# Second pair of attention heads ahead of retention, output projection cut along other tiles

## The chip, the cores and the metric

The kernel runs on one core of a Trainium2 chip. The metric is the device time of one execution in microseconds. Five engines take part: PE (TensorE, matrix products; PEld is its weight load), DVE (VectorE), ACT (ScalarE), POOL (GpSimd) and SP (SyncE, which issues nearly all DMAs). Each engine works through its own queue of instructions in order.

## The reference

Two layers over 512 tokens of width 1024, in float32. Each layer is a SwiGLU, a mixer and a second SwiGLU. The mixer projects the normalised tokens once and feeds four mixers of width 256, whose outputs are joined and projected by `w_out`:

```python
for l in range(DEPTH):
    x = x + 0.5 * swiglu(rmsnorm(x, ffn1_norm[l]), ffn1_w_gate[l], ffn1_w_up[l], ffn1_w_down[l])
    h = rmsnorm(x, mix_norm[l])
    u = h @ w_in[l]
    ...
    y_conv = short_conv_mixer(c_x, c_b, c_c, conv_w[l])
    y_rwkv = rwkv7_mixer(rw_r, rw_k, rw_v, ...)
    y_ret = retention_mixer(rt_q, rt_k, rt_v, rt_g, positions, ret_gn_g[l])
    y_mla = mla_mixer(ml_qa, ml_kva, positions, ...)
    x = x + jnp.concatenate([y_conv, y_rwkv, y_ret, y_mla], axis=-1) @ w_out[l]
    x = x + 0.5 * swiglu(rmsnorm(x, ffn2_norm[l]), ffn2_w_gate[l], ffn2_w_up[l], ffn2_w_down[l])
```

`rwkv7_mixer` is a recurrence over the tokens in both directions, `retention_mixer` a decayed attention in chunks with a normalisation at its end, `mla_mixer` a softmax attention of four heads.

## The kernel before

Activations lie feature by feature: a tile is 128 features by 512 tokens, and x is eight such tiles. Every large product is made of three products of rounded parts (`mm3`, L341): a weight block is split into a high and a low part (`split`, L326: one ACT copy, one DVE subtraction), and so is an activation (`y_split`, L638). The joined mixer output is eight tiles: 0 and 1 convolution, 2 and 3 RWKV, 4 and 5 retention, 6 and 7 attention. The weights `wo` of the output projection are stored in the order of `WOUT`, that is 0, 1, 4, 5, 2, 3, 6, 7.

`Mixers.run` (L552) writes the parts down in this order: the RWKV inputs and inverse, the RWKV recurrence (`rwkv_chain`, L1161), then everything that has nothing to do with it: the latents, the inputs of retention, the convolution, the inputs of attention, heads 0 and 1 (`mla(0)`), retention, the normalisation of the RWKV output (`rwkv_norm`, L1264), x brought back from DRAM (`x_back`, L590), the normalisation of retention (`retention_end`, L784), heads 2 and 3 (`mla(1)`), the RWKV output turned round (`rwkv_out`, L1295), and the output projection in two halves: weight columns 0 to 3, which are convolution and retention, and then 4 to 7, which are RWKV and attention.

The recurrence has eight steps. One step is a string of short products on PE with DVE or ACT between them: scores (L1187) and mask (L1191), old state (L1206), values (L1209), a copy (L1213), the solve (L1218), a negated copy (L1221), the new state (L1233, L1242, L1243), outputs (L1251, added by L1258).

One head of `mla` (L894) makes four score tiles (L909), each followed by a maximum and a scaling on DVE (L911, L912), an exponential on ACT (L914), a reciprocal and a scaling on DVE (L915, L916); then 16 transposes (L921) and copies (L922). The products with the values of both heads come after that (L929).

The order in which instructions stand in the engines' queues isn't the order of the source. It is planned when the kernel is built: of the instructions that could start, the one written earlier goes first, so that the parts written after `rwkv_chain` fill its waits; `in_turn` (L579) and `issue_after` pin an order, and the splits of weights carry a higher priority (`AHEAD`, L330). Tiles come from rings of buffers, one ring for each tag: SBUF has `v` (19 buffers), `f` (23), `h` (8) and `w_raw` (3); PSUM has `mm` (3), `a` (2) and `b` (3). The plan hands out the buffers of one ring in the order in which the source first writes the tiles: a tile never takes its buffer before a tile of the same ring that is written earlier in the source. The tags of `mla` are one line (scores, transposes, values of each head):

```python
MLA_TAGS = (("mm", "mm", "mm"), ("mm", "mm", "mm"), ("b", "a", "mm"), ("b", "a", "mm"))   # L28
```

The recurrence takes its scores and transposes from `a` and its products `zy` from `b`. Retention takes all its PSUM tiles from `mm`, its masked scores `ret_ms` from `f`, and two of the three `w_raw` buffers for each of its two halves (`ret_big`, `ret_big2`: decay tables, states). The attention output `m_y` and the transposed weights `m_pT` come from `f`.

Of the kernel before, what the change touches and what calls it, by code (L numbers as in the profile page):

```python
# [9 lines left out]
F32R = mybir.dt.float32r  # L10
# [5 lines left out]
P = 128  # L16
D = 1024
KD = D // P
# [27 lines left out]
WOUT = [0, 1, 4, 5, 2, 3, 6, 7]  # L46
# [498 lines left out]
class Mixers:  # L545
# [6 lines left out]
    def run(self):  # L552
        k, l, nc = self.k, self.l, self.nc
        self.xs = xs = k.dr.tile([P, KD, T], F32, name="xs")
        for d in range(KD):
            nc.sync.dma_start(xs[:, d], k.x[d])
        self.y = [None] * KD
        self.rwkv_in()
        self.rwkv_inverse()
        self.rwkv_bonus()  # L560
        self.rwkv_chain()
        self.latents()
        self.retention_in()
        self.conv()
        self.latents_end()
        self.mla_in()
        self.mla(0)
        for j in range(2):
            self.y_split(j, self.yc[j], k.vt(f"ys{j}", dt=F32R))
        self.retention()  # L570
        self.rwkv_norm()
        self.x_back()
        self.retention_end()
        self.mla(1)
        self.rwkv_out()
        self.w_out(lambda d: (0, 4))
        self.w_out(lambda d: (4, KD), ("ffn2_norm", l))

    def in_turn(self, calls):  # L579

# [60 lines left out]
        self.nc.vector.tensor_tensor(hl[:, 1], y, hl[:, 0].bitcast(F32), ALU.subtract)  # L641
        self.y[i] = hl

    def w_out(self, span, then=None):
        k, l, nc = self.k, self.l, self.nc
        for d in range(KD):
            a, b = span(d)
            raw = k.load(k.I["wo"][l, d][:, P * a:P * b], P * (b - a))
            hi, lo = k.split(raw, P * (b - a))
            ps = k.ps("po", "b" if then is None else "mm")  # L650
            for n in range(b - a):
                y = self.y[WOUT[a + n]]
                k.mm3(ps, hi[:, P * n:P * n + P], lo[:, P * n:P * n + P], y[:, 0], y[:, 1], n == 0, n == b - a - 1)
            nc.vector.tensor_tensor(k.x[d], ps, k.x[d], ALU.add)
            if then is not None:
                k.norm_part(d, *then)
# [237 lines left out]
    def mla(self, j):  # L894
        k, l, nc, V, A = self.k, self.l, self.nc, self.nc.vector, self.nc.scalar
        mm = nc.tensor.matmul
        ident = k.con("ident")
        fq, v = self.fq, self.mv
        y = k.ft("m_y")
        pTs = []  # L900
        for h in (2 * j, 2 * j + 1):
            e = h % 2
            qT, kT = self.qT[h], self.kT[j][:, e]
            tag = MLA_TAGS[h]
            pp = [k.ht("m_p") for _ in range(2)]
            for qt in range(NT):
                sl = slice(P * qt, P * qt + P)
                sc = k.ps("m_sc", tag[0])
                mm(sc, qT[:, sl], kT, start=True, stop=True)  # L909
                sm = k.tmp.tile([P, 4], F32, name="sm", tag="sm", bufs=3)  # L910
                V.tensor_reduce(sm[:, 0:1], sc, AX.X, ALU.max)  # L911
                V.tensor_scalar(sm[:, 1:2], sm[:, 0:1], fq[:, qt:qt + 1], -1.0, ALU.mult, ALU.mult)  # L912
                p = pp[qt // 2][:, qt % 2]
                A.activation(p, sc, AF.Exp, bias=sm[:, 1:2], scale=fq[:, qt:qt + 1], accum_out=sm[:, 2:3])  # L914
                V.reciprocal(sm[:, 3:4], sm[:, 2:3])  # L915
                V.tensor_scalar(p, p, sm[:, 3:4], None, ALU.mult)  # L916
            pT = [k.ft("m_pT") for _ in range(NT)]
            for kt in range(NT):
                pt = k.ps("m_ptp", tag[1])
                for qt in range(NT):  # L920
                    nc.tensor.transpose(pt[:, P * qt:P * qt + P], pp[qt // 2][:, qt % 2, P * kt:P * kt + P], ident)  # L921
                (A.copy if kt % 2 else V.tensor_copy)(pT[kt], pt)  # L922
            pTs.append(pT)

        po = k.ps("m_po", MLA_TAGS[2 * j + 1][2])

        def values(kt, e):
            o = N * (2 * j + e)
            return mm(po[64 * e:64 * e + 64], v[:, kt, o:o + N], pTs[e][kt], start=kt == 0, stop=kt == NT - 1)  # L929

        self.in_turn([(values, kt, e) for kt in range(NT) for e in range(2)])
        (A.copy if j else V.tensor_copy)(y, po)
        k.dump(f"ymla{j}_{l}", y)
        self.y_split(6 + j, y, k.vt(f"ys{6 + j}", dt=F32R))


    def rwkv_in(self):
# [466 lines left out]
```

## Time and profile before

| what | us |
|---|---|
| median of three runs (lowest, highest) | 2158.8 (2156.45, 2162.3) |
| the profiled execution's own time | 2154.35 |
| its span from first to last instruction | 2152.6 |
| PE busy in it | 2103.5 (98%) |
| DVE busy | 1412.9 (66%) |
| ACT busy | 893.0 (41%) |
| mean granted clock of PE | 0.99 |

The span is what the profile's rows divide; the execution's own time is 1.75 us more. The median of the runs is 4.45 us above the profiled execution. In the first layer the recurrence begins at about 537 us and ends at about 655 us, in the second at about 1605 and 1712 us; the output projection ends at about 721 and 1783 us. A busy PE means that a product was in flight, and matmuls overlap, so the column of idle time is the one to add up.

### The profile page before, as it was taken

What the parts mean: (1) busy time and instruction counts of PE and PEld (TensorE: products, weight loads), DVE (VectorE), ACT (ScalarE), POOL (GpSimd) and SP (SyncE); (2) the same over time, 40 slices, a digit from 0 to 9 for tenths busy, and PEclk for the clock granted to TensorE, in tenths of its full rate; (3) what the DMA queues carried; (4) which work ended last, traced back from release to release, by engine and by line L of the source; (5) the groups of instructions that cost most, each with busy time, mean ns of one, the idle gap of its engine ahead of it and who ended that gap; (6) DMA issues with size and microseconds to landing.
All of it is one profiled execution on the core that took longest, in us unless ns stands there. A gap on an engine that the chain in (4) does not pass through costs nothing.

```text
span 2152.6 us, 29873 instructions
## 1 busy us (share of the span) xinstructions
PE 2103.5 (98%) x11572; PEld 1705.7 (79%) x11572; DVE 1412.9 (66%) x2591; ACT 893.0 (41%) x1447; POOL 124.4 (6%) x146
## 2 busy tenths in 40 slices
PE   8999999999998999999999999999999999999997
PEld 6888888788665888888888888888886668888886
DVE  6785765676667676487557568657656766755763
ACT  5533543533323554254345344435324244533542
POOL 2000001000021100000100000010001201000001
PEclk9999999999999999999999999999999999999998
DMA  5233234234012323333332333342430223333332
GB/s 171 90 102 108 88 107 153 63 110 123 21 40 69 118 88 97 94 113 97 109 98 77 106 97 104 112 137 64 114 99 21 79 68 109 94 89 102 107 95 73
DMA packets 100014, 204.85 MB, mean 95 GB/s; under 512 B 30368, under 2 KB 30624, under 8 KB 99872
## 3 DMA queue, kind: packets, MB, share of 16 engines
q1 hardware_dynamic: 99872, 202.94, 31.2%
q8 instruction: 91, 1.49, 0.3%
q14 instruction: 51, 0.42, 0.1%
HBM read 191.37 MB, written 9.44 MB: 93 GB/s over the span
## 4 chain that ended last, share of the span: by engine, by line
PE 92%; DVE 4%; DMA 1%; ACT 1%; issue 1%; SPq 1%; DVEq 0%; ACTq 0%
PE pd L344 7%; PE pd L345 7%; PE pd L346 7%; PE pg L344 5%; PE pu L344 5%; PE pg L346 5%; PE pg L345 5%; PE pu L345 5%; PE pu L346 5%; PE f_y L427 4%; PE pj L344 4%; PE pj L346 4%; PE pj L345 4%; PE f_z L427 3%; PE f_y L429 2%; PE f_z L429 1%
## 5 line engine op out<-in xcount | busy, mean ns | idle before, releaser
L333 ACT CAST w_hi<-w_raw 128x512 fp32r<-128x512 f32 (+4 forms) x384 | 300.3, 797 | 600.4 <-PE pd L345 237.4
L334 DVE TENSOR_TENSOR w_lo<-w_raw,w_hi 128x512 fp32r<-128x512 f32 (+4 forms) x384 | 350.7, 921 | 245.9 <-ACT w_hi L333 245.0
L344 PE MATMUL pd<-g,w_hi 128*128 128x512 f32 x704 | 273.5, 389 | 1.1 <-DVE t L522 1.1
L345 PE MATMUL pd<-g,w_hi 128*128 128x512 f32 x704 | 273.9, 389 | 0.0
L346 PE MATMUL pd<-g,w_lo 128*128 128x512 f32 x704 | 273.9, 389 | 0.0
L404 ACT CAST w_hi<-w_raw 128x512 fp32r<-128x512 f32 x160 | 98.5, 621 | 204.5 <-PE pu L345 74.7
L344 PE MATMUL pg<-xg,w_hi 128*128 128x512 f32 x448 | 176.3, 393 | 6.3 <-ACT w_hi L333 6.3
L345 PE MATMUL pg<-xg,w_hi 128*128 128x512 f32 x448 | 175.5, 392 | 0.3 <-DVE xg L279 0.3
L346 PE MATMUL pg<-xg,w_lo 128*128 128x512 f32 x448 | 175.0, 391 | 0.0
L344 PE MATMUL pu<-xg,w_hi 128*128 128x512 f32 x448 | 174.6, 390 | 0.1
L345 PE MATMUL pu<-xg,w_hi 128*128 128x512 f32 x448 | 174.6, 390 | 0.0
L346 PE MATMUL pu<-xg,w_lo 128*128 128x512 f32 x448 | 174.5, 389 | 0.0
L344 PEld LDWEIGHTS pd<-g,w_hi 128*128 128x128 f32 x704 | 132.1, 188 | 28.8 <-ACT w_hi L333 1.5
L346 PEld LDWEIGHTS pd<-g,w_lo 128*128 128x128 f32 x704 | 132.1, 188 | 27.5
L345 PEld LDWEIGHTS pd<-g,w_hi 128*128 128x128 f32 x704 | 132.1, 188 | 27.2
L294 POOL TENSOR_TENSOR acc<-acc,sq 128x512 f32<-128x512 f32 x48 | 67.0, 1395 | 1480.1 <-ACT sq L292 1479.6
L346 PE MATMUL pj<-xg,w_lo 128*128 128x512 f32 x368 | 145.6, 396 | 2.5 <-DVE w_lo L334 2.5
L344 PE MATMUL pj<-xg,w_hi 128*128 128x512 f32 x368 | 146.4, 398 | 0.7 <-DVE krn L635 0.7
L345 PE MATMUL pj<-xg,w_hi 128*128 128x512 f32 x368 | 145.6, 396 | 0.0
L522 DVE SCALAR_TENSOR_TENSOR t<-pd,rb 128x512 f32<-128x512 f32 x64 | 44.2, 691 | 111.4 <-PE pd L346 111.4
L405 DVE TENSOR_TENSOR w_lo<-w_raw,w_hi 128x512 fp32r<-128x512 f32 x160 | 109.3, 685 | 1.5 <-ACT w_hi L404 1.4
L503 DVE TENSOR_TENSOR g<-pu,s 128x512 f32<-128x512 f32 x56 | 38.7, 691 | 106.4 <-PE pu L346 103.6
(346 smaller groups left out, 4161.4 us busy)
## 6 DMA issues: line engine op xcount, KB each, us to landing
w_raw<-gu SPq DMA_DIRECT2D x111, 512.0 KB, 3.7
w_raw<-gu SPq DMA_DIRECT2D x130, 256.0 KB, 3.1
w_raw<-dn SPq DMA_DIRECT2D x64, 384.0 KB, 3.1
w_raw<-win SPq DMA_DIRECT2D x46, 512.0 KB, 3.7
w_raw<-dn SPq DMA_DIRECT2D x64, 320.0 KB, 2.9
w_raw<-wo SPq DMA_DIRECT2D x32, 256.0 KB, 2.8
xs<-x SPq DMA_DIRECT2D x16, 256.0 KB, 3.2
x<-xs SPq DMA_DIRECT2D x16, 256.0 KB, 5.2
```

Source lines behind the costliest of these rows:

```text
L294: nc.gpsimd.tensor_tensor(self.acc, self.acc, self.sq, ALU.add)
L333: self.split_hi = self.nc.scalar.copy(hi[:, s], raw[:, s])
L334: self.nc.vector.tensor_tensor(lo[:, s], raw[:, s], hi[:, s].bitcast(F32), ALU.subtract)
L344: T_.matmul(ps, hi, xh, start=start, stop=False)
L345: T_.matmul(ps, hi, xl, start=False, stop=False)
L346: T_.matmul(ps, lo, xh, start=False, stop=stop)
L404: A.copy(hi[:, z], t)
L405: V.tensor_tensor(lo[:, z], t, hi[:, z].bitcast(F32), ALU.subtract)
L427: nc.tensor.matmul(ps.rearrange("p (q t) -> p q t", q=2), hi[:, c], b[i], start=start and i == 0, stop=False, skip_group_check=True)
L429: nc.tensor.matmul(ps[:, 0:256], lo[:, c], b[i][:, 0], start=False, stop=i == 3, skip_group_check=True)
L503: V.tensor_tensor(g, pu, s, ALU.mult)
L522: V.scalar_tensor_tensor(t, pd, 0.5, rb, ALU.mult, ALU.mult)
```

## The change

`mla(1)` moves to the place behind `mla(0)`, ahead of retention, and hands out its result instead of splitting it at once. The splits of the convolution and attention outputs follow it and take their tiles from ring `h`, no longer from `v`. `w_out` takes a list of tiles of the stored order instead of a range: the first half is now stored tiles 0, 1, 6, 7 (convolution and attention), the second 2, 3, 4, 5 (retention and RWKV). Where the tiles of a half don't lie side by side, the weights come in two DMAs of half the size. `MLA_TAGS` is unchanged.

```diff
@@ Mixers.run
-        self.y = [None] * KD
+        self.y, self.ym = [None] * KD, []
...
         self.mla(0)
+        self.mla(1)
         for j in range(2):
-            self.y_split(j, self.yc[j], k.vt(f"ys{j}", dt=F32R))
+            self.y_split(j, self.yc[j], k.ht(f"ys{j}", dt=F32R))
+            self.y_split(6 + j, self.ym[j], k.ht(f"ys{6 + j}", dt=F32R))
         self.retention()
         self.rwkv_norm()
         self.x_back()
         self.retention_end()
-        self.mla(1)
+        self.w_out((0, 1, 6, 7))
         self.rwkv_out()
-        self.w_out(lambda d: (0, 4))
-        self.w_out(lambda d: (4, KD), ("ffn2_norm", l))
+        self.w_out((2, 3, 4, 5), ("ffn2_norm", l))
@@ Mixers.w_out
-    def w_out(self, span, then=None):
+    def w_out(self, tiles, then=None):
         k, l, nc = self.k, self.l, self.nc
+        n = len(tiles)
         for d in range(KD):
-            a, b = span(d)
-            raw = k.load(k.I["wo"][l, d][:, P * a:P * b], P * (b - a))
-            hi, lo = k.split(raw, P * (b - a))
+            raw = k.raw()[:, :P * n]
+            a = 0
+            while a < n:
+                b = a + 1
+                while b < n and tiles[b] == tiles[b - 1] + 1:
+                    b += 1
+                nc.sync.dma_start(raw[:, P * a:P * b], k.I["wo"][l, d][:, P * tiles[a]:P * (tiles[b - 1] + 1)])
+                a = b
+            hi, lo = k.split(raw, P * n)
             ps = k.ps("po", "b" if then is None else "mm")
-            for n in range(b - a):
-                y = self.y[WOUT[a + n]]
-                k.mm3(ps, hi[:, P * n:P * n + P], lo[:, P * n:P * n + P], y[:, 0], y[:, 1], n == 0, n == b - a - 1)
+            for i, q in enumerate(tiles):
+                y = self.y[WOUT[q]]
+                k.mm3(ps, hi[:, P * i:P * i + P], lo[:, P * i:P * i + P], y[:, 0], y[:, 1], i == 0, i == n - 1)
@@ Mixers.mla
         (A.copy if j else V.tensor_copy)(y, po)
         k.dump(f"ymla{j}_{l}", y)
-        self.y_split(6 + j, y, k.vt(f"ys{6 + j}", dt=F32R))
+        self.ym.append(y)
```

## Rows read from the trace of the kernel before

**Rows 1.** The page, part 4: by engine, the chain that ended last.

```profile
PE 92%; DVE 4%; DMA 1%; ACT 1%; issue 1%; SPq 1%; DVEq 0%; ACTq 0%
```

**Rows 2.** Windows, first layer: start and end, length, then busy us of each engine.

```profile
core 0: us, PE busy (x) PEld busy (x) DVE busy (x) ACT busy (x) POOL busy (x), PEclk, DMA share, GB/s
575.00:613.30 38.30, 37.41 (x365) 24.49 (x364) 27.02 (x66) 16.61 (x39) 5.50 (x12) 1.00 0.01 1
...
654.40:668.80 14.40, 10.56 (x31) 4.78 (x31) 13.88 (x46) 6.06 (x15) 1.59 (x1) 0.88 0.13 49
...
613.30:699.60 86.30, 76.59 (x553) 51.32 (x553) 64.73 (x168) 25.08 (x52) 13.51 (x15) 0.96 0.22 68
```

**Rows 3.** Windows, second layer, the same columns.

```profile
1712.50:1732.10 19.60, 12.97 (x41) 6.25 (x42) 19.41 (x62) 8.40 (x21) 1.71 (x1) 0.83 0.08 32
...
1679.00:1760.80 81.80, 73.78 (x528) 49.84 (x525) 62.97 (x165) 25.26 (x52) 12.75 (x14) 0.96 0.22 72
```

**Rows 4.** Windows of 5 us, both layers; PEclk is the third number from the end.

```profile
630.00:635.00 5.00, 5.00 (x60) 3.86 (x60) 4.22 (x12) 0.62 (x1) 1.81 (x3) 0.66 0.20 59
...
655.00:660.00 5.00, 5.00 (x15) 2.41 (x15) 4.55 (x15) 0.00 (x0) 0.00 (x0) 0.66 0.29 109
1722.00:1727.00 5.00, 1.12 (x4) 0.58 (x4) 5.00 (x13) 1.41 (x3) 0.00 (x0) 0.67 0.00 0
1727.00:1732.00 5.00, 4.53 (x15) 2.16 (x13) 4.90 (x20) 3.50 (x9) 0.00 (x0) 0.65 0.00 0
...
585.00:590.00 5.00, 4.27 (x59) 3.32 (x59) 3.53 (x10) 1.65 (x5) 0.00 (x0) 1.00 0.00 0
```

**Rows 5.** Timeline of TensorE, first layer, from first pair to retention.

```profile
611.33 1.93 PE L929 MATMUL m_po<-m_pT,m_v 128*64 128x512 f32 x6
613.19 0.66 PE L737 MATMUL ret_pt<-con_t,ro_t 128*128 128x128 f32 x4
...
629.95 0.69 PE L1233 MATMUL zy<-ch 128*64 128x64 f32 x16 [2.45 <-DVE ch L1221]
```

**Rows 6.** Timeline of TensorE, first layer, last two chain steps: start, us, line, count, idle before.

```profile
643.62 0.68 PE L1218 MATMUL zy<-ch,NR 64*64 64x64 f32 x16
644.94 0.69 PE L1233 MATMUL zy<-ch 128*64 128x64 f32 x16 [0.63 <-DVE ch L1221]
...
647.15 0.71 PE L1206 MATMUL zy<-Sd,KQ 128*128 128x128 f32 x4
...
649.29 1.13 PE L909 MATMUL m_sc<-m_kT,m_qT 128*128 128x512 f32 x2
651.86 0.68 PE L1218 MATMUL zy<-ch,NR 64*64 64x64 f32 x16 [1.45 <-DVE ch L1213]
653.71 0.69 PE L1251 MATMUL zy<-ch,Gm 128*64 128x64 f32 x16 [1.17 <-DVE ch L1221]
```

**Rows 7.** Timeline of TensorE, second layer, last chain step.

```profile
1706.85 0.71 PE L1206 MATMUL zy<-Sd,KQ 128*128 128x128 f32 x4
...
1709.01 1.10 PE L909 MATMUL m_sc<-m_kT,m_qT 128*128 128x512 f32 x2
```

**Rows 8.** Windows of retention's score tile ret_ps alone, first layer.

```profile
613.30:699.60 86.30, 6.68 (x32) 3.65 (x32) 5.67 (x16) 0.96 0.22 68
```

**Rows 9.** Windows of retention's output tile ret_po alone, first layer.

```profile
613.30:699.60 86.30, 9.06 (x40) 3.58 (x40) 1.37 (x2) 1.18 (x2) 0.96 0.22 68
```

**Rows 10.** Windows of the score tile m_sc alone, second pair, first layer.

```profile
613.30:699.60 86.30, 10.17 (x16) 3.11 (x16) 5.46 (x8) 6.93 (x16) 0.96 0.22 68
```

**Rows 11.** Timeline of SP's DMA queue, first layer.

```profile
623.07 0.33 SPq L732 DMA_DIRECT2D ret_big<-big  x1
623.49 10.64 SPq L339 DMA_DIRECT2D w_raw<-wo  x3
```

**Rows 12.** The page, part 6: loads of the output projection's weights.

```profile
w_raw<-wo SPq DMA_DIRECT2D x32, 256.0 KB, 2.8
```

**Rows 13.** Windows of the projection tile po alone, first layer, in steady flow.

```profile
700.00:720.00 20.00, 20.00 (x90) 16.53 (x89) 5.33 (x8) 1.00 0.45 133
```

## The prediction

> **What bounds the kernel now.** I read the chain that ended last first: 92% of it is PE [rows 1], so a change of order gains only what PE loses by waiting. Then the windows, to see how much that is in the stretch that the change touches: from the last value product of heads 0 and 1 to the first product of the output projection that needs RWKV. That is 86.3 us in the first layer, of which PE is busy 76.59, so it waits 9.71 us [rows 2]; in the second 81.8 us with 73.78 busy, 8.02 us of waiting [rows 3]. The reader should also see how dense the stretch ahead is, where the recurrence is filled with heads 0 and 1: 37.41 of 38.3 us [rows 2].
>
> A second loss hides in busy time. After a stretch with long waits the granted clock reads 0.65 to 0.67, a mix of 1.2 and 2.4 GHz [rows 4]. In the first layer two windows of 5.00 busy us at 0.66 cost 2 x 5.00 x 0.34 = 3.4 us, in the second 1.12 x 0.33 + 4.53 x 0.35 = 2.0 us. So the change plays for 9.7 + 3.4 = 13.1 us in the first layer and 8.0 + 2.0 = 10.0 us in the second, 23.1 us together. Everything else there is work that any order has to do: 86.3 - 13.1 = 73.2 and 81.8 - 10.0 = 71.8 us.
>
> Last the timeline, for who comes when. Retention begins on PE the moment heads 0 and 1 are through [rows 5] and fills the recurrence's last steps. The first score of heads 2 and 3 comes at 649.29, right behind the last step's products with the old state and the values [rows 6]; in the second layer again, at 1709.01 behind 1706.85 [rows 7]. This is no accident: their scores take ring `b`, and so do the products of the recurrence, which are written earlier in the source. The plan never lets a tile overtake in its ring, so no score of heads 2 and 3 can stand ahead of the last step, whatever their place in the source.
>
> **The change part by part.** *Heads 2 and 3 earlier.* Their scores stay behind the last step, as above. What the move does change is what is behind them. Their value product `m_po` comes from ring `mm`, and now every PSUM tile of retention comes after it in that ring; `m_y` comes from ring `f`, and retention's masked scores come after it. So retention can't start its transposes before the first value product of heads 2 and 3, nor mask a score before their result is copied. Heads 2 and 3 start where they did, at the last step, and retention, which ran ahead of it, now runs after them. The stretch falls into three phases, and the sum is its work plus what PE waits in each.
>
> *Phase A, the last three steps with nothing beside them.* Before, retention's scores (6.68 us) and outputs (9.06 us) [rows 8, 9] lay here. The cover gone, the waits for the copies show. Between the last two solves lie 651.86 - 643.62 = 8.24 us, in which PE waited 0.63 + 1.45 us, and the last output waited 1.17 us more [rows 6]; L1206 waits for the new state too, though outputs cover most of that. The next step's scores and transposes still fill a little, and DVE has less to do. I take 1.5 us of waiting a step, nearer to the 2.08 us of that row than to nothing: 3 x 1.5 = 4.5 us. Bounds: 3 x 0.6 = 2 us and 3 x 2.6 = 8 us. In return the recurrence ends some 20 us earlier: 15.7 us of retention and most of 2.45 + 0.63 us of waits [rows 6, 5] leave it.
>
> *Phase B, heads 2 and 3 alone.* Eight scores, each with a maximum of 0.68 us on DVE and an exponential of 0.87 us on ACT [rows 10], a pipeline through three buffers. The nearest row is the same work before: 654.4 to 668.8 holds most of it, and PE waits 14.40 - 10.56 = 3.84 us there with DVE busy 13.88 us; in the second layer 19.60 - 12.97 = 6.63 us [rows 2, 3]. Retention's normalisation leaves DVE, but RWKV's stays, and the transposes and value products, which lay among products of the projection, stand bare. I take 3.5 us; bounds 1.5 and 7.
>
> *Phase C, retention and the first half of the projection.* The first half needs only convolution and heads, so it is meant to fill here. But its weights share the three `w_raw` buffers with retention. Before, the first weights were issued at 623.49, just behind retention's second half's table at 623.07 [rows 11], when the first half had let its buffers go, some 10 us after it started at 613.19 [rows 5]. After the change these 10 us begin only with heads 2 and 3 and finish behind them: masks, outputs, release, then a load of 2.8 us [rows 12], a cast and a subtraction. Until then PE has retention alone: half its outputs, a quarter to a half of its scores, the start of its second half, some 8 us of work in about 11. The second weight comes through one buffer, another 4 us or so later, with retention's second half and four products of three beside it. I take 5 us; bounds 1.5 (if weights come early) and 9.
>
> *Clock.* Waits of this kind brought 2.0 and 3.4 us of it before; I take 3, bounds 0 and 6.
>
> *Edits with one answer.* The projection has the same products; which tiles are in which half costs nothing by itself. The splits are as many; now in a row behind heads 2 and 3, on DVE, and the two late ones are in phase C. Ring `h` has eight buffers, of which heads 2 and 3 hold at most seven, so the splits wait for none that matters; ring `v` gains four, which brings x back earlier, and it wasn't late. SP gets eight more DMAs a layer, each 0.33 us to issue [rows 11], 2.6 us in all, at 128 KB instead of 256 KB. In steady flow a weight has 12 products, which take 12 x 20.00 / 90 = 2.7 us [rows 13], against three buffers in flight, which hides the issue; uncovered it costs 2.6 us a layer, and the first one may land up to 0.4 us late, which is inside phase C's bounds. No wait is added to SP that a load of the stretch behind stands after: the next weights, of the second half, come in the old order.
>
> **The sum.** A layer: 4.5 + 3.5 + 5 + 3 = 16 us of waiting and clock, against 13.1 and 10.0: 2.9 + 6.0 = 8.9 us slower. The profiled execution of 2154.35 us becomes 2163.3; it stood 4.45 us under the median of the runs, 2158.8, so the median goes to about 2168. All bounds low give 5 us a layer, 23.1 - 10 = 13 us faster; all high give 30, 37 us slower.
>
> **The rivals.** *Faster: the fill works.* If PE finds work in every phase (scores early in the last step, weights for the first half loaded beside heads 2 and 3), waits fall to the low ends, 2 + 1.5 + 1.5 + 0.5 = 5.5 us a layer: 23.1 - 11 = 12 us gained, about 2147. It decides at phase C: the first projection product has to come within 2 or 3 us of `m_y`. For it: heads 0 and 1 run beside the recurrence with 0.89 us of waits in 38.3 [rows 2], and the recurrence ends some 20 us earlier, which takes RWKV's normalisation off the end. Against it: the rings, by the rows of both layers [rows 6, 7], and the order of loads [rows 11]. Chance 0.22.
>
> *Same: one wait for another.* The waits that go and the waits that come are sums of the same kind of hand-off, 23.1 us against 2 x 12 = 24 if phases A and C each come out 2 us shorter than taken: about 2159. Nothing in the rows forbids it. Chance 0.28.
>
> *Slower by the clock.* Bare steps and bare scores may keep PE at the lower level through phases A and B. The row against it: 585 to 590 has 4.27 busy of 5 us and a clock of 1.00, so waits under 1 us don't lower it; for it: each of the four windows at 0.65 to 0.67 stands in or behind long waits [rows 4]. At the lower level for half of A and B's 40 us a layer, with half of it bound by products, 10 us of it a layer stand in place of 3: 2 x 23 - 23.1 = 23 us slower, about 2182. The Trainium skill, "TensorE: Matmul & The Clock Gate", section "HAM oscillation — how this bites in real kernels", says that an engine that waits between bursts again and again keeps falling to the lower clock and advises to group the bursts; by that rule, which speaks against taking the fill away, this case would be the likeliest, and the trace agrees with it only for waits of 2 us and more. Chance 0.1, as part of slower.
>
> **How the numbers follow.** My forecast, slower by the rings, has 0.4, the clock 0.1, the same 0.28, faster 0.22. The time is the forecast's, 2168. The forecast's own range is 2162 to 2179. For 8 in 10 the range takes in the same and most of the clock's case and the near half of the faster one: 2148 to 2184. A measurement of this kernel can tell about 0.3% from no change, 6.5 us: faster 0.22, same 0.28, slower 0.5.
>
> **What would show it.** Right: retention's first transpose (L737) behind the first score of heads 2 and 3 in both layers; the recurrence ending near 634 instead of 655; waits of about 0.5 to 1 us at L1218 and L1233 in its last steps; the first `po` product 10 us or more behind `m_y`. Wrong: retention's products between the steps as before, or scores of heads 2 and 3 ahead of the last step; a stretch of 86 us that shrinks below 80; PE busy through phase C. If the granted clock reads under 0.8 from 615 to 650, the clock's rival was right.

## The result and the profile after

The kernel after takes 2168.85 us (median of five runs, 2166.34 to 2170.55), the kernel before 2156.45 in the same number of runs: a ratio of 1.0064, 95% interval [1.0045, 1.0082]. The change costs about 0.6%. The profiled execution stands at 2170.26 us with a span of 2168.5, 15.9 us over the span of before. In the larger groups of runs that stand beside the experiments, before has a median of 2154.35 to 2154.82; against these the cost is some 14 us, against the five runs 12.4.

The chain that ended last, by engine, answers to [rows 1]: PE has lost two points, DVE and ACT have gained them.

```profile
PE 90%; DVE 5%; ACT 2%; DMA 1%; issue 1%; SPq 1%; DVEq 0%; POOL 0%; ACTq 0%
```

The windows answer to [rows 2, 3]; the cuts are those of the three phases of the prediction. Each line has start and end, length, the busy us of each engine, then the granted clock of PE.

```profile
core 0: us, PE busy (x) PEld busy (x) DVE busy (x) ACT busy (x) POOL busy (x), PEclk, DMA share, GB/s
575.00:614.40 39.40, 38.51 (x375) 25.16 (x375) 27.16 (x66) 16.60 (x39) 5.16 (x12) 1.00 0.01 1
614.40:635.20 20.80, 16.23 (x213) 13.28 (x212) 16.76 (x43) 2.65 (x7) 9.60 (x13) 0.85 0.14 43
635.20:664.10 28.90, 24.35 (x125) 11.97 (x124) 23.85 (x71) 12.09 (x27) 1.54 (x1) 0.87 0.16 53
664.10:673.80 9.70, 9.31 (x59) 5.20 (x59) 4.49 (x10) 1.85 (x4) 1.27 (x1) 1.00 0.18 54
614.40:706.60 92.20, 82.68 (x555) 55.70 (x554) 65.77 (x169) 25.38 (x52) 12.41 (x15) 0.93 0.21 66
1682.50:1704.50 22.00, 15.52 (x199) 12.68 (x196) 17.07 (x43) 2.86 (x7) 8.91 (x12) 0.84 0.16 47
1704.50:1735.00 30.50, 23.70 (x125) 11.05 (x124) 23.68 (x69) 12.47 (x27) 1.26 (x1) 0.95 0.13 45
1735.00:1744.70 9.70, 9.30 (x59) 5.19 (x59) 4.49 (x10) 1.85 (x4) 1.26 (x1) 1.00 0.19 56
1682.50:1777.30 94.80, 81.12 (x540) 54.01 (x538) 65.64 (x166) 26.08 (x52) 11.44 (x14) 0.95 0.21 65
```

Read length minus PE busy. In the first layer the recurrence's last three steps wait 20.80 - 16.23 = 4.57 us, heads 2 and 3 another 4.55, and the 9.7 us behind them, up to the first projection product, only 0.39. In the second layer it is 6.48, 6.80 and 0.40. The stretch ahead is as dense as in [rows 2], with 0.89 us of waits.

The clock in windows of 5 us, as [rows 4]:

```profile
625.00:630.00 5.00, 2.40 (x46) 1.80 (x46) 4.51 (x8) 1.26 (x3) 3.38 (x3) 0.89 0.00 2
630.00:635.00 5.00, 4.79 (x40) 4.11 (x40) 4.53 (x19) 0.00 (x0) 0.00 (x0) 0.50 0.37 105
635.00:640.00 5.00, 4.50 (x39) 2.57 (x36) 2.54 (x7) 1.61 (x4) 0.00 (x0) 0.50 0.84 276
640.00:645.00 5.00, 4.27 (x9) 1.72 (x9) 4.49 (x11) 0.93 (x3) 0.00 (x0) 0.74 0.11 42
1695.00:1700.00 5.00, 2.70 (x40) 2.24 (x42) 4.28 (x19) 1.14 (x3) 1.27 (x1) 0.73 0.00 0
1700.00:1705.00 5.00, 5.00 (x39) 4.19 (x36) 3.54 (x8) 0.37 (x1) 0.00 (x0) 0.50 0.60 180
1705.00:1710.00 5.00, 4.45 (x35) 1.87 (x34) 2.31 (x6) 1.25 (x3) 0.00 (x0) 0.75 0.68 240
```

PE is busy 2.40 of 5 us from 625 to 630, then the clock reads 0.50, the lower level, for 10 us. Busy time times what is missing to 1.00 is 0.3 + 2.4 + 2.25 + 1.1 = 6.0 us of loss in the first layer, and in the same way 4.3 in the second (1695 to 1710).

Who comes when, on TensorE (start, us, line, tile, count, wait and who ended it; the lines of the mixers are 9 further down than in before). This answers to [rows 5, 6]:

```profile
628.25 0.34 PE L1242 MATMUL zy<-ch 128*64 128x64 f32 x4 [1.18 <-DVE ch L1230]
...
634.16 1.11 PE L1218 MATMUL zy<-ch,Gm 64*64 64x64 f32 x14
635.20 2.07 PE L918 MATMUL m_sc<-m_kT,m_qT 128*128 128x512 f32 x2
...
651.51 1.07 PE L938 MATMUL m_po<-m_pT,m_v 128*64 128x512 f32 x2
652.51 0.65 PE L746 MATMUL ret_pt<-con_t,ro_t 128*128 128x128 f32 x4
...
664.17 0.70 PE L779 MATMUL ret_po<-ret_big,ret_big 128*128 128x256 f32 x2 [0.68 <-ACT m_y L941]
...
673.75 0.58 PE L344 MATMUL po<-ys,w_hi 128*128 128x512 f32 x1
```

No work of retention stands between the steps any more. The first score of heads 2 and 3 (L918) comes at 635.20, right behind the last step's products with the values (L1218). Retention's first transpose (L746), which stood at 613.19 in [rows 5], comes at 652.51, behind the first value product of heads 2 and 3 (L938), and its outputs wait for the copy of `m_y` (L941).

### The profile page after: what moved, and what is told of

The parts are those of the page before. It is cut to its first block, busy times and chain, and to the rows that moved or that the text cites. A ratio compares the mean times of both kernels' runs of the same rounds, so it can differ in the third digit from the quotient of the medians.

```text
span 2168.5 us, 29895 instructions
## 1 busy us (share of the span) xinstructions
PE 2114.7 (98%) x11572; PEld 1711.8 (79%) x11572; DVE 1416.5 (65%) x2591; ACT 891.9 (41%) x1447; POOL 122.6 (6%) x146
## 4 chain that ended last, share of the span: by engine, by line
PE 90%; DVE 5%; ACT 2%; DMA 1%; issue 1%; SPq 1%; DVEq 0%; POOL 0%; ACTq 0%
PE pd L344 7%; PE pd L345 7%; PE pd L346 7%; PE pg L344 5%; PE pu L344 5%; PE pg L346 5%; PE pg L345 5%; PE pu L346 5%; PE pu L345 5%; PE f_y L427 4%; PE pj L344 4%; PE pj L346 4%; PE pj L345 4%; PE f_z L427 3%; PE f_y L429 2%; PE f_z L429 1%
```

## The experiments

Theory R (rings) is the prediction's: the order in which rings hand out buffers keeps the scores of heads 2 and 3 behind the recurrence and now retention behind heads 2 and 3, so the last steps and the heads both run bare. Rival P (place): the cost lies in where things are written or in the new halves, whatever the rings. Each ratio is to before's runs beside it (medians 2154.35, 2154.82 and 2154.70 in the three groups; for after, 2156.45).

| run | us | ratio, 95% interval | stretches, us | between, us |
|---|---|---|---|---|
| before | | | 146.4 + 140.8 | 920.4 |
| after | 2168.85 | 1.0064 [1.0045, 1.0082] | 151.7 + 152.6 | 918.3 |
| e1_all_mm | 2152.00 | 0.9983 [0.9970, 0.9996] | 142.4 + 145.3 | 918.5 |
| e2_move_only | 2179.91 | 1.0119 [1.0105, 1.0132] | 157.4 + 158.7 | 916.6 |
| e3_halves_only | 2156.31 | 1.0008 [0.9998, 1.0017] | 149.6 + 141.9 | 918.1 |
| e4_tables_in_v | 2175.22 | 1.0100 [1.0084, 1.0115] | 156.2 + 151.0 | 920.9 |
| e5_free_retention | 2162.98 | 1.0036 [1.0018, 1.0053] | 151.0 + 149.9 | 914.5 |
| e6_all_mm_act_copies | 2158.36 | 1.0014 [1.0001, 1.0027] | 139.6 + 141.8 | 928.8 |
| e7_all_mm_tables_in_v | 2157.37 | 1.0005 [0.9992, 1.0018] | 144.3 + 139.6 | 918.4 |
| e8_before_all_mm | 2162.43 | 1.0031 [1.0019, 1.0042] | 146.7 + 144.3 | 923.0 |
| e9_rings_freed | 2166.63 | 1.0054 [1.0037, 1.0072] | 149.7 + 148.5 | 922.0 |
| e10_all_free | 2146.29 | 0.9963 [0.9950, 0.9975] | 137.3 + 140.5 | 920.6 |
| e11_all_mm_again | 2152.57 | 0.9991 [0.9980, 1.0002] | 142.7 + 143.5 | 918.7 |

The last two columns are read from the timeline of each profiled execution. A stretch goes from the first score of head 0 to the last product of the projection, in the first and in the second layer; "between" goes from there to the first score of the second layer, in code that no edit touches. The same kernel profiled twice (e1, e11) differs by under 2 us in each stretch and by 0.2 us between them. From kernel to kernel the part between the layers moves by up to 14 us, so a median that differs by a few us need not come from the edited stretch.

**1. Let the scores of heads 2 and 3 out of the recurrence's ring** (after, one line):

```diff
-MLA_TAGS = (("mm", "mm", "mm"), ("mm", "mm", "mm"), ("b", "a", "mm"), ("b", "a", "mm"))
+MLA_TAGS = (("mm", "mm", "mm"),) * 4
```

> The changed kernel with all four heads in PSUM ring mm (MLA_TAGS). Rings theory: scores of heads 2 and 3 no longer stand behind the recurrence in ring b, so their first one follows the value products of heads 0 and 1 at once (near 615 us in the first layer, ahead of the last three steps), retention follows them, and PE's waits plus half-clock loss in the stretch fall from 15 to 18 us a layer to about 8: 2150 us (2144 to 2158), faster than the changed kernel by 0.5 to 1.1% and than the kernel before by up to 0.6%. Rival (heads 2 and 3 are bound by their own string of softmax steps, whatever their ring): 2163 us or more.

2152.0 us: the whole loss is gone with one line, which moves the scores out of ring `b` and the transposes out of ring `a`. The timeline shows scores (L918) and transposes (L930) of heads 2 and 3 between the recurrence's steps, and retention's first transpose at 646.17:

```profile
626.36 0.71 PE L1215 MATMUL zy<-Sd,KQ 128*128 128x128 f32 x4
...
627.25 1.98 PE L918 MATMUL m_sc<-m_kT,m_qT 128*128 128x512 f32 x4
...
646.17 0.66 PE L746 MATMUL ret_pt<-con_t,ro_t 128*128 128x128 f32 x4
```

So the new place in the source costs nothing once these tiles have another ring. The scores alone decide most of it: experiment 6 differs from the run before it by their ring only, and by 20 us. Before has its scores in ring `b` too and no such loss, so the loss needs both the move and the ring (experiment 7). Taken again beside the last group, the same kernel gave 2152.57 (e11_all_mm_again), so that a gain over before stays at the edge of what can be told.

> The kernel after with all heads in ring mm, as measured before (2152.0, ratio 0.9983), once more beside the two above: 2148 to 2155, and a ratio to before of 0.996 to 1.000.

**2 and 3. One part of the change alone.** The move with the old halves:

```diff
-        self.w_out((0, 1, 6, 7))
+        self.w_out((0, 1, 2, 3))
...
-        self.w_out((2, 3, 4, 5), ("ffn2_norm", l))
+        self.w_out((4, 5, 6, 7), ("ffn2_norm", l))
```

> The changed order, but the halves of the projection as before (convolution and retention first). Rings theory: the bare steps and the bare heads stay, waits as in the changed kernel; and now nothing of the projection can stand beside retention and its normalisation, so PE waits some 4 to 8 us a layer more: 2178 to 2185 us. Rival (the new halves cost the time, the move none): back to about 2157 us.

2179.91 us, as R had it. The move alone costs 25.6 us, and the new halves give back some 11 of them: a first half of convolution and attention can run before retention's normalisation is through. In this run that chain stands bare, with a wait of 3.03 us ahead of its broadcast (L260) that after doesn't have.

The halves without the move (before, with after's `w_out`; `mla(1)` stays behind `retention_end`):

```diff
+        self.y_split(6, self.ym[0], k.vt("ys6", dt=F32R))
...
+        self.y_split(7, self.ym[1], k.vt("ys7", dt=F32R))
+        self.w_out((0, 1, 6, 7))
-        self.w_out(lambda d: (0, 4))
-        self.w_out(lambda d: (4, KD), ("ffn2_norm", l))
+        self.w_out((2, 3, 4, 5), ("ffn2_norm", l))
```

> The order of before (heads 2 and 3 behind retention), with the new halves. Rings theory: retention fills the last steps again (clock near 1.00 there), but the first half now waits for heads 2 and 3, which stand bare from about 655 us; PE waits some 4 to 7 us a layer more than before: about 2168 us (2161 to 2174). Rival (the new halves gain by themselves): under 2154 us.

Neither: 2156.31, no change that can be told. The expectation held the late attention tile against the halves, but the products of a half need their tiles one by one, and those of the convolution fill the heads' waits from 669.27 on, as this run's timeline of TensorE shows:

```profile
669.27 0.48 PE L344 MATMUL po<-ys,w_hi 128*128 128x512 f32 x1
```

**4. Weights of the first half earlier** (after, retention's tables out of `w_raw`):

```diff
-            big, big2 = k.raw("ret_big"), k.raw("ret_big2")
+            big, big2 = (k.vt(n, shape=(P, 1024)) for n in ("ret_big", "ret_big2"))
```

> The changed kernel with retention's tables in ring v instead of w_raw, so that weights of the projection can be loaded and split beside heads 2 and 3. If the lag of the first weights cost what phase C was taken at (5 us a layer), 8 to 10 us faster than the changed kernel: about 2160 us. If retention alone kept PE busy in that lag, as the trace of the changed kernel reads (9.31 busy of 9.70 us), within 3 us of it: about 2168 us, with the first projection product some 8 us earlier.

Neither. The projection does start 20 us earlier, at 653.26 instead of 673.75, and the median is some 6 us higher. The fill is spent ahead of retention: its second half's state products (L754) come at 684.14 (in after at 670.71), and its normalisation, one short chain on DVE, is left bare at the end: PE waits 1.10 and 3.02 us. From the timeline of TensorE:

```profile
653.26 0.71 PE L344 MATMUL po<-ys,w_hi 128*128 128x512 f32 x2
...
684.14 0.69 PE L754 MATMUL ret_sp<-ret_v,ret_big 128*64 128x64 f32 x16
...
701.32 1.05 PE L802 MATMUL ret_ss<-con_t,ret_sq 128*128 128x2 f32 x8 [1.10 <-ACT ret_sq L789]
705.40 1.97 PE L260 MATMUL ret_pb<-con_t,ret_sq 128*128 128x128 f32 x8 [3.02 <-DVE ret_sq L257]
```

So the lag that the prediction charged with 5 us costs nothing: retention fills it by itself, and the projection is kept for later. That the bare tail is the whole of the 6 us isn't shown. In the profiled executions the first stretch is 4.5 us longer than after's and the second 1.6 us shorter; and in the last step, ahead of the tail, PE waits 2.34 and 2.74 us (633.81, 637.24) where after has no wait over 1.18 in the first layer. The same edit on the kernel with all heads in `mm`:

> All heads in ring mm, and retention's two tables in ring v instead of w_raw, so that the first half's weights can load at once. Theory (fill spent early): projection products run ahead of retention's second half, whose normalisation then stands bare at the end of the stretch, as in the kernel after with the tables in v (waits of 1.10 and 3.02 us before 701 and 705, and the lower clock behind them): 2155 to 2160, 3 to 8 us over the run without it (2152). Rival (there the loss lay in the bare steps ahead, not in the tail): 2150 to 2154, with no wait over 1 us between 690 and 710.

2157.37, inside the theory's range, and one wait behind 640 us in TensorE's timeline of the first stretch, the one named:

```profile
695.17 1.97 PE L260 MATMUL ret_pb<-con_t,ret_sq 128*128 128x128 f32 x8 [3.44 <-DVE ret_sq L257]
```

But the profiled execution, at 2150.23, is the fastest of the ten (up to 2161.21), and its stretches are no longer than those of experiment 1 (283.9 against 287.7 and 286.2 us). What raised the median isn't in this trace, so here the cost of early weights stays open.

**5. Is it retention's lateness that costs?** First, the value product and `m_y` out of retention's way:

```diff
-MLA_TAGS = (("mm", "mm", "mm"), ("mm", "mm", "mm"), ("b", "a", "mm"), ("b", "a", "mm"))
+MLA_TAGS = (("mm", "mm", "mm"), ("mm", "mm", "mm"), ("b", "a", "mm"), ("b", "a", "a"))
-        y = k.ft("m_y")
+        y = k.vt("m_y")[:, 0] if j else k.ft("m_y")
```

> The kernel after, with the value product of heads 2 and 3 in PSUM ring a and their result m_y in ring v, so that neither stands ahead of retention's tiles in its ring; the scores stay in ring b. By the rings (all that the move costs is the order in which buffers are handed out): retention comes back beside the last steps of the recurrence, first transpose near 613 in the first layer instead of 652.5; phase A's waits (4.6 and 6.5 us, and the half clock behind them) go, heads 2 and 3 run late with the first half's convolution products as fill, and the time is that of before's order with these halves, 2152 to 2159. By the rival (the place in the source or the new halves cost it, whatever the rings): retention still starts behind heads 2 and 3, or the time stays at 2164 or more.

2162.98: half of the expected gain, between the two expectations. Retention's first transpose is back at 617.4, but its masked scores (L776) still come behind heads 2 and 3, right behind the last copy of transposed probabilities in the timeline of VectorE:

```profile
660.52 0.69 DVE L931 COPY m_pT<-m_ptp 128x512 f32<-128x512 f32 x1 [1.21 <-PE m_ptp L930]
661.13 1.41 DVE L776 TENSOR_TENSOR ret_ms<-ret_ps,ret_big 128x256 f32<-128x256 f32 x4
```

`m_pT` comes from ring `f` too, as `ret_ms` does; the prediction had named `m_po` and `m_y` alone. So next all three rings were freed (the tags as above, `m_y` back in `f`, and `ret_ms`, `ret_o` and `ret_sq` in `v`):

```diff
-                ps, ms = [k.ps("ret_ps", "mm") for _ in range(2)], [k.ft("ret_ms") for _ in range(2)]
+                ps, ms = [k.ps("ret_ps", "mm") for _ in range(2)], (lambda w: (w[:, 0], w[:, 1]))(k.vt("ret_ms"))
...
-            o, sq = k.ft("ret_o"), k.ft("ret_sq")
+            o, sq = (lambda w: (w[:, 0], w[:, 1]))(k.vt("ret_o"))
```

> The kernel after with all three rings freed that keep retention behind heads 2 and 3: the value product of heads 2 and 3 in PSUM ring a, retention's masked scores and its outputs in ring v instead of f, where the transposed probabilities m_pT and m_y of heads 2 and 3 stand ahead of them (in the run that freed only m_po and m_y, the first masked score came at 661.13 us, right behind the last m_pT copy at 660.52). The place in the source, the halves and the scores in ring b stay as in after. By the rings: all of retention runs beside the recurrence again, its sums of squares (L802) by 650 in the first layer instead of 684 to 693, and the time is that of before's order with these halves, 2152 to 2159. By the rival (something else in the change costs it): 2164 or more though retention is early.

Retention is back beside the recurrence, its sums of squares through at 645.5, and the time is 2166.63, not 2156. The half of R that names retention has mostly fallen: with the scores still in ring `b`, bringing retention forward moves the median by 2.2 us, which is inside the noise, and the two stretches by 6.1 us (298.2 against 304.3). The window behind the recurrence shows what is left. PE waits 7.33 of 30 us there, at a clock of 0.89, with heads 2 and 3 and only the first products of the projection (the columns are those of the windows above):

```profile
655.00:685.00 30.00, 22.67 (x97) 14.30 (x97) 22.82 (x63) 12.07 (x26) 1.66 (x1) 0.89 0.00 1
```

On TensorE's timeline of the same run the longest of these waits stands ahead of a score and ends with ScalarE's exponential:

```profile
660.58 1.51 PE L918 MATMUL m_sc<-m_kT,m_qT 128*128 128x512 f32 x2 [3.93 <-ACT m_p L923]
```

ScalarE itself had waited 8.77 us there for VectorE's scaling (L921 at 659.43), and VectorE had put steps of both normalisations ahead of it (L1299 at 655.16, L1300 at 657.63, L808 at 658.23). So the retention work that covers the steps is taken from the heads, whose scores hang on DVE and ACT.

Why this run is not under the one that freed less is in the last two columns: its stretches are 2.7 us shorter, and the part between the layers is 7.5 us longer. Against experiment 3, which has the same halves, the same ring for the scores and retention ahead as well, its stretches are still 6.7 us longer. The two differ in where heads 2 and 3 stand in the source and in the rings of a few tiles (`ret_ms`, `ret_o`, `m_po` and the splits). So rival P is not excluded for this part. One piece of it is the wait of 3.04 us in the last section; the rest stays open.

**6. Both free** (as above, and the scores in `mm`):

```diff
-MLA_TAGS = (("mm", "mm", "mm"), ("mm", "mm", "mm"), ("b", "a", "mm"), ("b", "a", "a"))
+MLA_TAGS = (("mm", "mm", "mm"), ("mm", "mm", "mm"), ("mm", "a", "mm"), ("mm", "a", "a"))
```

> As the run with the rings freed, and the scores of heads 2 and 3 in mm as well (transposes stay in a): heads 2 and 3 and retention can both fill the recurrence's last steps. If hand-out order is what holds the stretch, PE has fill in every phase and the waits fall to 2 to 4 us a layer: 2143 to 2150. Rival (VectorE is the bound: 21.0 busy of 22.0 us from 613 to 635 with heads 2 and 3 alone beside the recurrence): no gain over all heads in mm, 2150 to 2156, with VectorE busy over 90% from 613 to 650.

2146.29, ratio 0.9963: faster than both kernels, 8.4 us under before, some 22 under after and 20.3 under the run above. The same window, the one ahead of it, and both with what follows:

```profile
613.00:655.00 42.00, 40.56 (x360) 24.75 (x360) 34.99 (x89) 16.15 (x35) 6.71 (x11) 1.00 0.09 30
655.00:685.00 30.00, 28.15 (x175) 22.12 (x174) 24.74 (x72) 6.88 (x13) 5.20 (x4) 1.00 0.46 148
613.00:706.00 93.00, 88.92 (x623) 63.21 (x622) 76.21 (x185) 34.75 (x67) 16.50 (x19) 1.00 0.27 85
```

4.08 us of waits in 93 us and the full clock all through. The rival named VectorE as the bound; it is 34.99 of 42 us busy (83%, and 83% from 613 to 650), not over 90%.

**7. Do the tags do it without the move?** (before, the line of experiment 1)

> The kernel before with MLA_TAGS all mm and nothing else. If the gain of the run with all heads in mm needs the move (heads 2 and 3 must stand ahead of retention in ring mm to fill the recurrence), heads 2 and 3 still come behind retention and the time is before's or worse, 2153 to 2165. If the rings alone make the gain, 2145 to 2151.

2162.43: no, they make before slower. With `mla(1)` written behind retention, ring `mm` keeps its scores behind all of retention's tiles: four of the eight score tiles come at 679 us and later, against 667.7 for the last one in before. The four kernels, with and without the move, with and without the ring, show that the two belong together: ring alone 2162.43, move alone 2168.85, both 2152.00, neither 2154.35 to 2154.82 (the two with the move have the new halves as well).

**8. Less for VectorE** (experiment 1, the copies of heads 2 and 3 all on ScalarE):

```diff
-                (A.copy if kt % 2 else V.tensor_copy)(pT[kt], pt)
+                (A.copy if j or kt % 2 else V.tensor_copy)(pT[kt], pt)
```

> All heads in ring mm, and for heads 2 and 3 all eight copies of the transposed probabilities on ScalarE instead of four on VectorE. In the run with all heads in mm VectorE is busy 21.0 of 22.0 us from 613 to 635 and 4.91 of 5 us from 633 to 638, with ScalarE at 12 of 22. By the theory that VectorE is the bound of that stretch: 4 copies of 0.69 us go, so 2 to 3 us a layer and some of the half clock behind, 2144 to 2149 against that run's 2152. By the rival (the hand-offs of the recurrence bound it, VectorE is merely busy): 2151 to 2154.

2158.36, a miss for both. In both stretches its profile shows a gain. In the first layer, from the first score of head 0 to the last projection product, it takes 717.0 - 577.4 = 139.6 us, against 715.5 - 573.1 = 142.4 in experiment 1; in the second 141.8 against 145.3; and the clock from 613 to 706 reads 1.00 instead of 0.96. It is lost between the layers: from there to the first score of the second layer 928.8 us instead of 918.5, in code that the edit doesn't touch. From 1440 to 1640 PE waits 6.36 us instead of 4.70, and the clock is 0.96 instead of 0.97, which is not all of it. Why wasn't settled.

## Why the prediction was right, step by step

The forecast, slower by the rings, gave 2168 us, and it is 2168.85. The way and the path were right; that the figure lies within 1 us is luck. The base of the forecast, the median of three runs of before, was 2158.8 and is 2156.45 over five, so the change measured is 12.4 us (15.9 between the profiled executions) where 8.9 was forecast. And inside the sum several errors cancel.

- **Heads 2 and 3 start where they did, and retention runs behind them: right** on both counts (635.20 and 652.51; in the second layer 1704.49 and 1722.54). Experiment 1 undoes the first with one line, experiment 5 the second. The reason given for retention was incomplete: `m_pT` holds ring `f` as well (experiment 5). And "the cover gone" was put down to retention; experiments 5 and 6 show that bringing retention forward is worth 2 to 6 us by the medians and 3 to 6 by the stretches, and the ring of the scores 16 to 20 (experiment 1, where the transposes change rings too, and experiment 6).
- **Phase A, 4.5 us a layer:** 4.57 and 6.48. Right in the first layer, inside the bounds in the second. Waits at L1227, L1242 and L1260 are 0.19 to 1.18 us in the first layer, and the longest in the second is 2.23. "DVE has less to do" was wrong: RWKV's normalisation now falls between the bare steps, and the copy that ended this longest wait (L1222) stood behind it in VectorE's queue, behind an operation (L1293) that took 1.08 us and ended with GpSimd's L1291 (1692.57 + 1.26). The timelines of the second layer, VectorE, then TensorE:

```profile
1692.78 1.08 DVE L1293 TENSOR_SCALAR gn_st<-gn_st 128x8 f32<-128x8 f32 x1
1693.96 0.69 DVE L1294 TENSOR_TENSOR gn_wk<-Yn,gn_st 128x512 f32<-128x512 f32 x1
1694.69 0.43 DVE L1222 COPY ch<-zy 64x256 f32<-64x256 f32 x1
```

```profile
1695.17 0.33 PE L1227 MATMUL zy<-ch,NR 64*64 64x64 f32 x2 [2.23 <-DVE ch L1222]
```

- **Phase B, 3.5 us:** 4.55 and 6.80, too low, in the bounds. The nearest rows [rows 2, 3] had 3.84 and 6.63; taking less than either, because retention's normalisation leaves DVE, was the error: DVE is still busy 23.85 of 28.90 us. The transposes that "stand bare" were named and given no price; PE waits 2.03 and 3.24 us for the copies of `m_pT` (L931) ahead of them, the largest part in both layers.
- **Phase C, 5 us: wrong, 0.39 and 0.40, under its lower bound of 1.5.** The step "half its outputs, a quarter to a half of its scores, the start of its second half, some 8 us of work in about 11" took retention for too little. From 664.1 to 673.8 PE finds 9.31 us of it in 9.70. The weights did come late, the first products at 673.75, 9.6 us behind `m_y`; that cost nothing, and with earlier weights the median of experiment 4 is 6 us higher.
- **Clock, 3 us: too low, 6.0 and 4.3, the first at its upper bound.** The prediction held that waits under 1 us don't lower the clock [rows 4, the window 585 to 590], and that before's trace shows a fall only behind waits of 2 us and more. Its own rows say otherwise: the window 655 to 660 at 0.66 [rows 4] stands behind waits of 1.45 and 1.17 us [rows 6]. Here no wait between 614 and 640 is over 1.18 us, and the clock reads 0.50 from 630 to 640. So the rule of the Trainium skill, "TensorE: Matmul & The Clock Gate", section "HAM oscillation — how this bites in real kernels", that an engine which idles between bursts falls back again and again, agrees with this trace for shorter waits than the prediction granted. Its rival (10 us a layer, 2182) still asked for twice what came.
- **The sum of waits and clock:** forecast 16 a layer, 32 in all; found 9.5 + 6.0 and 13.7 + 4.3, 33.5 in all (waits from 614.40 to 706.60 and 1682.50 to 1777.30). Against 23.1 before that is +10.4, forecast +8.9.
- **"Everything else is work that any order has to do": wrong by 7 us.** From the starts of [rows 2, 3] to the last projection product there were 107.8 and 103.3 us, now 112.9 and 115.7. Less waits and clock, the work has grown from 94.7 to 97.4 and from 93.3 to 97.7. The products are the same; groups that stand bare can't overlap their neighbours, which is the likely reason, argued and not isolated. The rest of the program gave 1.6 us back, and the profiled execution of after lies 1.4 us above its median.
- **Its signs.** Two came short: the recurrence ends near 640, not 634 (some 14 us earlier, not 20), since the 4.57 us that it now waits in its last steps were not taken off, and the first projection product stands 9.6 us behind `m_y`, not 10. One sign of being wrong did come: PE is busy through phase C, 9.31 of 9.70 us. And the sign of the clock's rival, a clock under 0.8 from 615 to 650, stands on its edge, at 0.80.

The rival "same" wanted phases A and C each 2 us shorter; C was 4.6 shorter, A no shorter than taken, and B, the clock and the work ate it. "Faster: the fill works" named phase C as the place that decides. It isn't: with the first projection product ahead of `m_y` (experiment 4) the kernel is slower still. What decides is whether heads 2 and 3 can start inside the recurrence, which that rival set aside by the rings, and rightly for this change.

## What to carry to other kernels

Before moving a block earlier in the source to use it as fill, list every ring it draws on, SBUF and PSUM, and what stands ahead of it and behind it in each: one shared tag can void the move, and one more can turn it into a gain (here 1.0064 against 0.9963). Fill is one pool: give the recurrence the part that is bound by other engines (softmax heads), and keep the dense products for the serial tails at the end. Work that arrives early is spent early: with earlier weights a bare tail of some 4 us a layer stood at the end (experiment 4), though how much of that reaches the time is open. And before a few us are put down to an edit, look whether they lie in the stretch that it touches.

## What the runs showed of the hardware

**Some VectorE operations are held until a GpSimd operation ends.** In the run with the rings freed, three VectorE operations on 128 x 8 elements, 0.17 us or less elsewhere, take 1.19 to 1.26 us each (the second and third lie in rows of two, with one of 0.16), and each ends with one of three GpSimd operations. The timelines of the second layer: GpSimd, then VectorE, then the TensorE solve that waited for the copy (L1222) queued behind them:

```profile
1718.59 1.26 POOL L1291 TENSOR_TENSOR gn_wk<-gn_wk,lg 128x512 f32<-128x512 f32 x1 [2.15 <-DMA lg<-lnx]
1719.81 1.27 POOL L1297 TENSOR_TENSOR gn_wk<-gn_wk,lg 128x512 f32<-128x512 f32 x1
1721.04 1.26 POOL L1291 TENSOR_TENSOR gn_wk<-gn_wk,lg 128x512 f32<-128x512 f32 x1
```

```profile
1718.53 0.17 DVE L239 TENSOR_SCALAR rq_v<-ret_ss 128x16 f32<-128x16 f32 x1
1718.62 1.26 DVE L239 TENSOR_SCALAR rq_v<-gn_st 128x8 f32<-128x8 f32 x1
1719.79 1.31 DVE L240 TENSOR_SCALAR rq_r<-rq_v 128x16 int32<-128x16 int32 x2
1721.02 1.31 DVE L241 TENSOR_SCALAR rq_r<-rq_r 128x16 int32<-128x16 int32 x2
...
1722.33 0.41 DVE L1222 COPY ch<-zy 64x256 f32<-64x256 f32 x1
```

```profile
1722.79 1.12 PE L1227 MATMUL zy<-ch,NR 64*64 64x64 f32 x16 [3.04 <-DVE ch L1222]
```

1718.59 + 1.26 = 1719.85 against 1718.62 + 1.26 = 1719.88, and so for the other two. Others are not held: in after, a reduction (L1292) and a copy out of PSUM (L1222) take their usual 0.69 and 0.43 us at 624.66 and 625.91, beside GpSimd operations that last longer. The wait of 1.45 us at the last solve in [rows 6], from which the prediction took its price for a bare step, has the same origin in before's trace: there L243 and L244 take 1.24 and 1.19 us. The Trainium skill, "GPSIMD Engine Reference", section "Specifications", says that GpSimd shares its SBUF interfaces with VectorE, and names VectorE instructions with two SBUF inputs or in a two-port mode as those that contend. The rows agree that there is a hold, and put it at the rest of the GpSimd operation. L243 and L244 have two SBUF inputs, as the page has it; the three of the run above have one, and whether they run in such a mode no row shows.

**The same order, the same waits, another clock.** At the start of the second layer the runs of experiments 5 and 6 issue the same products with the same waits. From the timelines of TensorE, first the run with the rings freed, then the one with both free:

```profile
1617.82 0.69 PE L1242 MATMUL zy<-ch 128*64 128x64 f32 x16 [0.80 <-DVE ch L1230]
1619.06 0.71 PE L1215 MATMUL zy<-Sd,KQ 128*128 128x128 f32 x4 [0.56 <-DVE Sd L1252]
1619.96 1.77 PE L250 MATMUL m_pb<-con_t,m_fckv 128*128 128x128 f32 x8
```

```profile
1605.31 0.69 PE L1242 MATMUL zy<-ch 128*64 128x64 f32 x16 [0.80 <-DVE ch L1230]
1606.55 0.71 PE L1215 MATMUL zy<-Sd,KQ 128*128 128x128 f32 x4 [0.56 <-DVE Sd L1252]
1607.45 1.16 PE L250 MATMUL m_pb<-con_t,m_fckv 128*128 128x128 f32 x8
```

The `m_pb` group takes 1.77 us in one and 1.16 in the other, though the two groups ahead are spaced and waited for alike; up to the first score the one takes 1647.44 - 1617.82 = 29.6 us, the other 1632.09 - 1605.31 = 26.8. The granted clock is what differs: in both runs the 10 us up to the `m_pb` group have 8.64 us of busy PE at 1.00, and the 10 us from there have 9.54 us at 0.52 in the first run and 0.83 in the second. What sets them apart isn't in these rows. The kernel of experiment 1, profiled twice, has its first score of head 0 at 573.1 and at 577.5 us. A few us between two single profiles are therefore no evidence by themselves; the verdicts above rest on the medians, and the two columns of stretches only say where a difference lies.
